# One decoder kernel: every low weight part on VectorE, the token norm's sums one step earlier, the decay products in one place, state keys scaled on ScalarE, two half output tiles placed among the last transposes

## Chip, cores and metric

The kernel runs on one core of a Trainium2 chip. The metric is the device time of one execution in microseconds, the median of several runs; lower is better. The engines are named as in the profile: PE (TensorE matrix products), PEld (its weight loads), DVE (VectorE), ACT (ScalarE), POOL (GpSimd) and SP (SyncE, which issues the transfers of weights).

## Reference

A decoder trunk of two layers on 512 tokens of width 1024, all in float32. Each layer adds three blocks to the residual stream:

```python
for layer in range(DEPTH):                       # DEPTH = 2
    x = x + 0.5 * swiglu(rmsnorm(x, norm_ffn1[layer]), ...)      # D_FF = 2816
    x = x + hybrid_mixer(rmsnorm(x, norm_mix[layer]), ...)
    x = x + 0.5 * swiglu(rmsnorm(x, norm_ffn2[layer]), ...)
return rmsnorm(x, norm_final)
```

The mixer makes one input projection and feeds three groups of heads: HGRN2 (a gated linear recurrence; q, forget gate f, value i and output gate g, 4 heads of 64), a gated delta rule (q, k, v through a causal convolution of 4 taps and SiLU, gates `g = -exp(a_log) * softplus(gd_a + dt_bias)` and `beta = sigmoid(gd_b)`, a triangular solve per chunk, 4 heads of 128), and RG-LRU (a scan). Their outputs are normed, gated, concatenated to 1024 columns and multiplied by `w_out`.

## The kernel before

**Products.** A float32 product is done as three products of split operands: each weight block has a high part `whi` and a low part `wlo`, each activation a high and a low part; `mm3_step` issues hi by hi (L212), hi by lo (L213) and lo by hi (L214), each 128x512. One weight unit (128 columns of outputs, 8 blocks of 128 inputs) is 24 such matmuls. Activations lie with features on partitions and the 512 tokens along the row.

**Weights.** SP loads a raw unit (`wraw`, three buffers). `_split` makes, for each half of a unit, `whi` by a copy on ACT (L176) and `wlo` by a subtraction (L177) on `self.lo_engine`: DVE in the feed-forward blocks, the value projection and the output projection, POOL during the rest of the mixer's input stage. A half is prepared one unit ahead of its use.

**Order.** In the mixer the order of PE is written by hand (`manual_schedule(engines={PE})`); the other engines' orders are made by the framework's scheduler. `Slots` runs a main list of projections, each of which yields a step after every 6 matmuls, and side lines (`sl.add`) that wait for an event and a number of steps: `("gd4", GAP)` resumes a line GAP steps after the projection of `gd4` is through. Whatever a line issues on PE when it is resumed stands at that place in PE's queue.

**The mixer's stages on PE.** (1) The value projection: 4 quarters q, tokens on partitions, 256 columns of HGRN2 values and 8 columns of gates into `pv` (L533 to L535). `rstd` (L293 and the small steps behind it) sums the squares for the norm's factor `rt`; `spread` (L304) puts it on all partitions as `rb` (L306), by which every projection's result is multiplied on DVE. (2) Projections gd4 to gd7 (keys), with a side line for the gates: `log1pexp` (L404 to L419, some 30 operations on 128x16, nearly all on DVE), L615 (three sums of g), L617 (their exponentials) and four decay products L626 with exponential (L628) and mask (L629); and a side line for the keys: transposes (L641), key products (L667, multiplied by DT on DVE, L668). When all four heads are through, L686 scales the result and `gdn_solve` sends its 16x16 blocks through DRAM and solves them on DVE (L745, L747, 15 pairs). (3) The two HGRN2 heads, hq1 first: L970 multiplies, L496 applies SiLU, and then come 8 levels of blocks (L1017 and L1004 on PE; L1022, L1008, L988 and L989 on DVE), the two heads alternating, with 6 matmuls of a projection between. (4) Convolved queries and values (L485, L492, L496; transposes again L641), merges of the solve (L777, L786), the chunk chain, gates. (5) The end: four transposes of the delta rule's output (L935), each multiplied (L505) and split (L235, L236) into parts of `Y`; then `mixer_out`, 8 output tiles of 24 matmuls, whose order over the parts of Y is `Y_ORDER = (0, 1, 6, 7, 2, 3, 4, 5)`.

`gtmp` tiles ("gt") have four buffers, PSUM banks "mm" and "mx" three each, "hx" two.

Of the kernel before, what the change touches and what calls it, by code (L numbers as in the profile page):

```python
# [5 lines left out]
F32 = mybir.dt.float32  # L6
# [106 lines left out]
class Trunk:  # L113
# [56 lines left out]
    def _split(self):  # L170
        raw, n = self.loaded[len(self.ready) // 2]
        o = n // 2 * (len(self.ready) % 2)
        hi = self.tile(self.wp, (P, NWU // 2), F32R, "whi")
        lo = self.tile(self.wp, (P, NWU // 2), F32R, "wlo")
        hi, lo, raw = hi[:, 0:n // 2], lo[:, 0:n // 2], raw[:, o:o + n // 2]
        self.nc.scalar.copy(hi, raw)  # L176
        self.lo_engine.tensor_tensor(lo, raw, hi.bitcast(F32), ALU.subtract)  # L177
        self.ready.append((hi, lo))
# [335 lines left out]
    def mixer_in(self, l):  # L514
# [8 lines left out]
        for q in range(4):  # L523
            w = self.weights()
            if q == 3:
                self.rt = self.rstd(0, NJ, "mx")
# [9 lines left out]
        self.lo_engine = nc.gpsimd  # L536

        def norm():
            for j in range(NJ):
                nc.vector.tensor_scalar(ba[:, j, :], pv[j][:, 256:264], self.rt[:, j:j + 1], None, ALU.mult)  # L540
            for j in range(NJ):
                nc.scalar.activation(HV[:, j, :], pv[j][:, 0:256], AF.Copy, scale=self.rt[:, j:j + 1])
            yield 1
            _, self.rb = self.spread(self.rt, NJ, "mm")
            sl.fire("rb")


        tl = lambda n, tag: self.tile(self.mp, (P, n), F32, tag)
        for line in (norm(), self.gdn_gates(l, ba), self.gdn_k(), self.gdn_q(), self.gdn_v(), self.gdn_core(),
# [9 lines left out]
        sl.run([(need and (need, 0), line) for _, need, line in main])  # L559

    def mixer_out(self, l, nxt):
        nc = self.nc
        self.lo_engine = nc.vector
# [31 lines left out]
    def gdn_gates(self, l, ba):  # L595
# [3 lines left out]
        yield ("rb", 0)  # L599
# [3 lines left out]
        nc.scalar.activation(v3(self.beta), ba[:, :, 0:4], AF.Sigmoid)  # L603
# [7 lines left out]
        nc.vector.tensor_tensor(v3(self.g), v3(sp), nea, ALU.mult)  # L611
        yield 7
# [9 lines left out]
        gm = None  # L622
        for c in range(NJ + 1):
            if c:
                pd = self.bank("mx")
                nc.tensor.matmul(pd, lhsT=self.gt, rhs=gm.rearrange("p a b -> p (a b)"), start=True, stop=True)  # L626
                dt = self.DT[:, 4 * c - 4:4 * c, :]
                nc.scalar.activation(dt.rearrange("p a b -> p (a b)"), pd, AF.Exp)  # L628
                nc.vector.tensor_tensor(dt, dt, self.le[:, None, :].to_broadcast([P, 4, P]), ALU.mult)  # L629
            if c < NJ:  # L630
                gm = self.gtmp()
                nc.vector.tensor_tensor(gm, self.le[:, None, :].to_broadcast([P, 4, P]),
                                        bc(self.g[:, 4 * c:4 * c + 4], P), ALU.mult)
                yield 1
# [17 lines left out]
    def gdn_k(self):  # L652
# [17 lines left out]
        for h in range(4):  # L670
# [254 lines left out]
    def gdn_out(self, l):  # L925
# [4 lines left out]
        yield 3  # L930
        for h in range(4):
            yield (f"z{h}", 0)
# [176 lines left out]
    def hgrn_out(self, l, V):  # L1109
# [4 lines left out]
        for i in range(2):  # L1114
# [6 lines left out]
            self.out_parts(i, pt.rearrange("p a b -> p (a b)"), self.hgg[i], self.par[:, c0 + C_HGW:c0 + C_HGW + 1])  # L1121

# [20 lines left out]
    def rglru(self, l):  # L1143
# [35 lines left out]
        for i in range(2):  # L1179
            self.parts(6 + i, bx[i])  # L1180


    def run(self):
        tc, nc, t = self.tc, self.nc, self.t
        from contextlib import ExitStack
        with ExitStack() as es:
# [8 lines left out]
            self.lo_engine = nc.vector  # L1195
# [64 lines left out]
GAP = 3  # L1260
# [78 lines left out]
```

## Time and profile before

| | |
|---|---|
| median of 3 runs | 2126.92 us (2125.84 to 2127.35) |
| the profiled execution | 2125.51 us, its span 2123.7 us |
| PE busy | 2074.2 us, 98% of the span |
| DVE, ACT, POOL busy | 1122.3, 807.3 and 159.6 us |
| mean granted TensorE clock | 0.991 of full speed |

The profile is of one execution. Busy time of PE counts matmuls whose ends are modelled, so waits of PE are read from the list of waits, which names for each group of waiting instructions who released it, and the stretches of lower clock from windows that give the granted clock (PEclk). In the timeline each row has its start, its duration, the engine, the line and operation, tiles and, in brackets, the idle time before it and its releaser.

### The profile page before, as it was taken

What the parts mean: (1) busy time and instruction counts of PE and PEld (TensorE: products, weight loads), DVE (VectorE), ACT (ScalarE), POOL (GpSimd) and SP (SyncE); (2) the same over time, 40 slices, a digit from 0 to 9 for tenths busy, and PEclk for the clock granted to TensorE, in tenths of its full rate; (3) what the DMA queues carried; (4) which work ended last, traced back from release to release, by engine and by line L of the source; (5) the groups of instructions that cost most, each with busy time, mean ns of one, the idle gap of its engine ahead of it and who ended that gap; (6) DMA issues with size and microseconds to landing.
All of it is one profiled execution on the core that took longest, in us unless ns stands there. A gap on an engine that the chain in (4) does not pass through costs nothing.

```text
span 2123.7 us, 26758 instructions
## 1 busy us (share of the span) xinstructions
PE 2074.2 (98%) x10292; PEld 1681.8 (79%) x10292; DVE 1122.3 (53%) x1996; ACT 807.3 (38%) x1519; POOL 159.6 (8%) x148
## 2 busy tenths in 40 slices
PE   8999999899999999999999999998899999999997
PEld 6888888778778788888888888887688778888886
DVE  6434445686475543444644343457855754444445
ACT  5323224544464332323433232346345543223233
POOL 0000000332230000000000000003312200000000
PEclk9999999999999999999999999999999999999998
DMA  5232222221113223232223232222211222322222
GB/s 182 91 98 95 94 98 77 85 71 45 51 60 96 93 90 100 90 99 91 98 90 100 90 100 90 94 79 85 66 41 51 70 90 99 92 98 93 96 90 70
DMA packets 67488, 184.99 MB, mean 87 GB/s; under 512 B 18976, under 2 KB 21920, under 8 KB 67360
## 3 DMA queue, kind: packets, MB, share of 16 engines
q1 hardware_dynamic: 66128, 182.12, 26.9%
q8 instruction: 81, 1.33, 0.2%
q10 hardware_dynamic: 1232, 1.16, 0.2%
q14 instruction: 47, 0.39, 0.1%
HBM read 180.36 MB, written 2.88 MB: 86 GB/s over the span
## 4 chain that ended last, share of the span: by engine, by line
PE 92%; DVE 6%; ACT 1%; DMA 0%; issue 0%; SPq 0%; DVEq 0%; ACTq 0%
PE mm L212 13%; PE mm L213 12%; PE mm L214 12%; PE mx L212 8%; PE mx L214 8%; PE mx L213 8%; PE hx L212 8%; PE hx L214 8%; PE hx L213 8%; DVE tmp L492 1%; PE hx L1004 1%; PE mx L641 1%; PE hx L1059 0%; DVE r_q L911 0%; PE hx L1062 0%
## 5 line engine op out<-in xcount | busy, mean ns | idle before, releaser
L176 ACT CAST whi<-wraw 128x512 fp32r<-128x512 f32 (+2 forms) x696 | 420.2, 606 | 983.7 <-PE mm L213 330.6
L177 DVE TENSOR_TENSOR wlo<-wraw,whi 128x512 fp32r<-128x512 f32 (+2 forms) x592 | 393.6, 666 | 316.2 <-ACT whi L176 315.3
L212 PE MATMUL mm<-xh,whi 128*128 128x512 f32 x1120 | 462.5, 413 | 6.6 <-ACT whi L176 6.6
L213 PE MATMUL mm<-xl,whi 128*128 128x512 f32 x1120 | 443.7, 396 | 0.0
L214 PE MATMUL mm<-xh,wlo 128*128 128x512 f32 x1120 | 443.4, 396 | 0.0
L212 PE MATMUL mx<-xh,whi 128*128 128x512 f32 x704 | 279.5, 397 | 0.0
L214 PE MATMUL mx<-xh,wlo 128*128 128x512 f32 x704 | 278.6, 396 | 0.0
L213 PE MATMUL mx<-xl,whi 128*128 128x512 f32 x704 | 277.0, 394 | 0.0
L212 PE MATMUL hx<-y,whi 128*128 128x512 f32 x692 | 273.0, 395 | 0.0
L213 PE MATMUL hx<-y,whi 128*128 128x512 f32 x692 | 272.1, 393 | 0.0
L214 PE MATMUL hx<-y,wlo 128*128 128x512 f32 x692 | 272.1, 393 | 0.0
L212 PEld LDWEIGHTS mm<-xh,whi 128*128 128x128 f32 x1120 | 212.6, 190 | 56.8 <-ACT whi L176 6.6
L214 PEld LDWEIGHTS mm<-xh,wlo 128*128 128x128 f32 x1120 | 212.4, 190 | 50.9 <-DVE wlo L177 0.2
L213 PEld LDWEIGHTS mm<-xl,whi 128*128 128x128 f32 x1120 | 213.1, 190 | 47.0 <-issue 3.4
L177 POOL TENSOR_TENSOR wlo<-wraw,whi 128x512 fp32r<-128x512 f32 x104 | 142.5, 1374 | 358.7 <-ACT whi L176 350.3
L214 PEld LDWEIGHTS mx<-xh,wlo 128*128 128x128 f32 x704 | 132.6, 188 | 32.6 <-issue 0.7
L213 PEld LDWEIGHTS mx<-xl,whi 128*128 128x128 f32 x704 | 132.8, 189 | 30.7 <-issue 0.2
L212 PEld LDWEIGHTS mx<-xh,whi 128*128 128x128 f32 x704 | 132.4, 188 | 31.1 <-issue 1.0
L214 PEld LDWEIGHTS hx<-y,wlo 128*128 128x128 f32 x692 | 130.1, 188 | 31.0
L213 PEld LDWEIGHTS hx<-y,whi 128*128 128x128 f32 x692 | 130.2, 188 | 30.6 <-DVE y L236 1.0
L212 PEld LDWEIGHTS hx<-y,whi 128*128 128x128 f32 x692 | 130.0, 188 | 29.5
L359 DVE SCALAR_TENSOR_TENSOR x<-hx,x 128x512 f32<-128x512 f32 x94 | 65.0, 692 | 132.8 <-PE hx L214 132.8
(328 smaller groups left out, 1910.4 us busy)
## 6 DMA issues: line engine op xcount, KB each, us to landing
wraw<-in_wgu SPq DMA_DIRECT2D x176, 512.0 KB, 3.7
wraw<-in_wd SPq DMA_DIRECT2D x64, 512.0 KB, 3.5
wraw<-in_win SPq DMA_DIRECT2D x52, 512.0 KB, 3.5
wraw<-in_wd SPq DMA_DIRECT2D x32, 384.0 KB, 3.0
wraw<-in_wout SPq DMA_DIRECT2D x16, 512.0 KB, 3.5
wraw<-in_wv SPq DMA_DIRECT2D x8, 264.0 KB, 2.5
x<-in_x SPq DMA_DIRECT2D x3, 512.0 KB, 7.9
out_dram<-xw SPq DMA_DIRECT2D x4, 256.0 KB, 2.5
```

The source lines that it names most:

```text
L176: self.nc.scalar.copy(hi, raw)
L177: self.lo_engine.tensor_tensor(lo, raw, hi.bitcast(F32), ALU.subtract)
L212: nc.tensor.matmul(ps, lhsT=a, rhs=xh, start=(n == 0), stop=False)
L213: nc.tensor.matmul(ps, lhsT=a, rhs=xl, start=False, stop=False)
L214: nc.tensor.matmul(ps, lhsT=b, rhs=xh, start=False, stop=(n == size - 1))
L359: nc.vector.scalar_tensor_tensor(xm, pd, 0.5, xm, ALU.mult, ALU.add)
L492: nc.vector.scalar_tensor_tensor(c, pad[:, 1 + i:1 + i + S], w[i], c, ALU.mult, ALU.add)
L641: self.nc.tensor.transpose(ps[:, c, :], v[:, c * P:(c + 1) * P], self.ident)
L1004: nc.tensor.matmul(banks[e][:, j], lhsT=k[r, j * P:(j + 1) * P], rhs=half(q)[r, j], start=True, stop=True)
```

## The change

1. `wlo` is always made on VectorE. Before, 104 halves (52 in each layer's mixer) were made on POOL.
2. `rstd` stands at the third quarter of the value projection (q == 2) and not at the fourth; `spread`, the scaling of the gate columns (`ba`) and of the HGRN2 values (`HV`) follow the projection at once and not in a side line one step later; the gates' line no longer waits for an event.
3. The decay products: all four masked tiles `gm` are computed right behind g, the four products stand together behind L615, and beta's sigmoid is issued behind them.
4. The keys that go into the states are scaled on ACT as they leave PSUM (three activations for each head), in place of a copy on ACT and three multiplications per layer on POOL (L694).
5. GAP is 4 and not 3; the delta rule's output line starts one step later and each of its heads waits 3 steps behind its gate z.
6. `out_first`, twice: the first 12 matmuls (parts 0, 1, 6, 7 of Y) of output tiles 0 and 1 go into the main list as soon as these parts are there (event "y"); `mixer_out` finishes the two tiles.

The number of matmuls is the same. The diff, cut to its core:

```diff
-        self.lo_engine.tensor_tensor(lo, raw, hi.bitcast(F32), ALU.subtract)
+        self.nc.vector.tensor_tensor(lo, raw, hi.bitcast(F32), ALU.subtract)
...
-            if q == 3:
+            if q == 2:
                 self.rt = self.rstd(0, NJ, "mx")
...
-        self.lo_engine = nc.gpsimd
-
-        def norm():
-            for j in range(NJ):
-                nc.vector.tensor_scalar(ba[:, j, :], pv[j][:, 256:264], self.rt[:, j:j + 1], None, ALU.mult)
-            for j in range(NJ):
-                nc.scalar.activation(HV[:, j, :], pv[j][:, 0:256], AF.Copy, scale=self.rt[:, j:j + 1])
-            yield 1
-            _, self.rb = self.spread(self.rt, NJ, "mm")
-            sl.fire("rb")
+        _, self.rb = self.spread(self.rt, NJ, "mm")
+        for j in range(NJ):
+            nc.vector.tensor_scalar(ba[:, j, :], pv[j][:, 256:264], self.rt[:, j:j + 1], None, ALU.mult)
+        for j in range(NJ):
+            nc.scalar.activation(HV[:, j, :], pv[j][:, 0:256], AF.Copy, scale=self.rt[:, j:j + 1])
...
+        main += [(("y", 0), self.out_first()) for _ in range(2)]
+        sl.run(main)
+
+    def out_first(self):
+
+        ps, w = self.bank(), self.weights()
+        for n in range(KT // 2):
+            self.mm3_step(ps, w, self.Y, n, KT, Y_ORDER[n])
+            if n % 2:
+                yield
+        self.first.append((ps, w))
...
-            ps = self.bank()
-            self.mm3(ps, self.weights(), self.Y, Y_ORDER)
+            if m < len(self.first):
+                ps, w = self.first[m]
+                for n in range(KT // 2, KT):
+                    self.mm3_step(ps, w, self.Y, n, KT, Y_ORDER[n])
+            else:
+                ps = self.bank()
+                self.mm3(ps, self.weights(), self.Y, Y_ORDER)
...
-        nc.scalar.activation(v3(self.beta), ba[:, :, 0:4], AF.Sigmoid)
...
+        gm = []
+        for c in range(NJ):
+            gm.append(self.gtmp())
+            nc.vector.tensor_tensor(gm[c], self.le[:, None, :].to_broadcast([P, 4, P]),
+                                    bc(self.g[:, 4 * c:4 * c + 4], P), ALU.mult)
         yield 7
...
-        gm = None
-        for c in range(NJ + 1):
...
+        for c in range(NJ):
+            pd = self.bank("mx")
+            nc.tensor.matmul(pd, lhsT=self.gt, rhs=gm[c].rearrange("p a b -> p (a b)"), start=True, stop=True)
+            dt = self.DT[:, 4 * c:4 * c + 4, :]
+            nc.scalar.activation(dt.rearrange("p a b -> p (a b)"), pd, AF.Exp)
+            nc.vector.tensor_tensor(dt, dt, self.le[:, None, :].to_broadcast([P, 4, P]), ALU.mult)
+        nc.scalar.activation(v3(self.beta), ba[:, :, 0:4], AF.Sigmoid)
         sl.fire("DT")
...
-            nc.scalar.copy(hc(self.Kn)[:, h], ps[:, 0:NJ - 1, :])
             yield ("DT", 1)
+            for c in range(NJ - 1):
+                nc.scalar.activation(self.Kn[:, 4 * c + h, :], ps[:, c, :], AF.Copy,
+                                     scale=self.ex[:, 1, 4 * c + h:4 * c + h + 1])
...
-        for c in range(NJ - 1):
-            cs = slice(4 * c, 4 * c + 4)
-            kd = self.Kn[:, cs, :]
-            nc.gpsimd.tensor_tensor(kd, kd, bc(self.ex[:, 1, cs], P), ALU.mult)
...
-        yield 3
+        yield 4
         for h in range(4):
-            yield (f"z{h}", 0)
+            yield (f"z{h}", 3)
...
+        yield ("hgy", 0)
+        self.sl.fire("y")
...
-GAP = 3
+GAP = 4
```

Where this moves instructions is seen in the engines' queues. First PE around the gates, before: L615 sums g, "mx" are PSUM banks, "gt" the masked tiles, and a "..." stands for three more rows of the same projection.

```order
L214 MATMUL mm_3158<-xh_91,wlo_3107 128x512
L615 MATMUL mx_3175<-g_3079,cst_87 128x16 x3
L212 MATMUL mm_3158<-xh_91,whi_3106 128x512
L213 MATMUL mm_3158<-xl_92,whi_3106 128x512
L214 MATMUL mm_3158<-xh_91,wlo_3107 128x512
...
L626 MATMUL mx_3192<-gt_3184,cst_87 128x512
L212 MATMUL mm_3158<-xh_91,whi_3110 128x512
L213 MATMUL mm_3158<-xl_92,whi_3110 128x512
L214 MATMUL mm_3158<-xh_91,wlo_3111 128x512
...
L626 MATMUL mx_3204<-gt_3196,cst_87 128x512
```

The same place after; L628 is the former L615, L637 the former L626, L648 the key transposes that were L641.

```order
L214 MATMUL mm_3110<-xh_91,wlo_3024 128x512
L628 MATMUL mx_3154<-g_3068,cst_87 128x16 x3
L637 MATMUL mx_3163<-gt_3070,cst_87 128x512
L637 MATMUL mx_3167<-gt_3072,cst_87 128x512
L637 MATMUL mx_3171<-gt_3074,cst_87 128x512
L637 MATMUL mx_3175<-gt_3076,cst_87 128x512
L648 MATMUL mx_3180<-cst_87,y_596_3100 128x128 x4
L212 MATMUL mm_3190<-xh_91,whi_3113 128x512
```

Before, the first key transposes stood 30 projection matmuls behind L304 and L615 12 matmuls behind them, with the four decay products after it, 6 matmuls apart; after, L304 is followed by 48 projection matmuls, then L615's successor, the four products in a row and the first transposes.

The second place is DVE ahead of the first HGRN2 level, before: L683 and L686 belong to the delta rule's solve, L961, L991 and L970 to head hq1.

```order
L683 TENSOR_TENSOR bk_3396<-bk_3396,beta_3043 128x16
L961 TENSOR_SCALAR gd_v_3365<-gd_v_3365 128x512
L686 TENSOR_TENSOR y_575_3027<-y_575_3027,bk_3396 128x512 x4
L991 TENSOR_TENSOR hg_tot_3632<-gd_v_3365 128x256
L970 TENSOR_TENSOR gd_v_3365<-mm_3492,rb_3041 128x512
L991 TENSOR_TENSOR hg_tot_3673<-hg_tot_3632 128x128
```

The same place after (L975 was L970, L692 was L683, L695 was L686).

```order
L697 SCALAR_TENSOR_TENSOR ik_3428<-ksq_3080,rk_3404 128x16
L975 TENSOR_TENSOR gd_v_3360<-mm_3378,rb_3006 128x512
L692 TENSOR_TENSOR bk_3421<-bk_3421,beta_3033 128x16
L177 TENSOR_TENSOR wlo_3597<-wraw_3535,whi_3596 128x512
L695 TENSOR_TENSOR y_592_3078<-y_592_3078,bk_3421 128x512 x4
L177 TENSOR_TENSOR wlo_3601<-wraw_3535,whi_3600 128x512
L1027 TENSOR_TENSOR gd_v_3360<-hx_3564,cst_87 128x512
```

hq1's multiplication now stands ahead of the four scalings of the solve, and halves of `wlo` stand among them. Further on, in the levels, DVE has this piece after (L1013 was L1008, L750 and L752 were L745 and L747):

```order
L1013 COPY_PREDICATED hg_s_703_3585<-cst_87,hx_3749 128x256
L752 TENSOR_TENSOR gt_3441<-gt_3441,solve_3474 128x5x11
L492 SCALAR_TENSOR_TENSOR tmp_3742<-tmp_3739,par_76,tmp_3742 128x512
L750 TENSOR_TENSOR solve_3477<-gt_3430,gt_3441 128x4x12
L492 SCALAR_TENSOR_TENSOR tmp_3742<-tmp_3739,par_76,tmp_3742 128x512
L752 TENSOR_TENSOR gt_3441<-gt_3441,solve_3477 128x4x12
L492 SCALAR_TENSOR_TENSOR tmp_3742<-tmp_3739,par_76,tmp_3742 128x512
L750 TENSOR_TENSOR solve_3480<-gt_3430,gt_3441 128x3x13
L1013 COPY_PREDICATED hg_s_704_3586<-cst_87,hx_3750 128x256
```

Before, the two copies of a level (L1008) of this head stood next to each other, or with one solve step between; here three steps of a convolution stand between them too.

The third place is PE's end of the mixer, before: the last transposes L935 and the first output tile, whose operands are parts of Y (`y_...`).

```order
L214 MATMUL mm_5322<-xh_91,wlo_5275 128x512
L935 MATMUL mx_5359<-cst_87,r_q_3733 128x128 x4
L212 MATMUL mm_5369<-y_976_5092,whi_5325 128x512
L213 MATMUL mm_5369<-y_976_5092,whi_5325 128x512
L214 MATMUL mm_5369<-y_976_5092,wlo_5326 128x512
```

The same place after (L940 was L935); the "..." stands for the other rows of the first half of tile 0.

```order
L214 MATMUL mm_5318<-xh_91,wlo_5271 128x512
L212 MATMUL mm_5364<-y_976_5097,whi_5321 128x512
...
L212 MATMUL mm_5387<-y_976_5097,whi_5367 128x512
L213 MATMUL mm_5387<-y_976_5097,whi_5367 128x512
L214 MATMUL mm_5387<-y_976_5097,wlo_5368 128x512
...
L940 MATMUL mx_5404<-cst_87,r_q_3738 128x128 x4
L212 MATMUL mm_5387<-y_1000_5219,whi_5367 128x512
```

The last transposes stood ahead of all 192 matmuls of the output stage; now 18 of these stand ahead of them. The first L935 of a layer, which stood 36 projection matmuls behind the chunk chain's last products, stands 48 behind them.

## Rows read from the trace of the kernel before

**Rows 1.** The page: busy time (us), share and instruction count of each engine.

```profile
PE 2074.2 (98%) x10292; PEld 1681.8 (79%) x10292; DVE 1122.3 (53%) x1996; ACT 807.3 (38%) x1519; POOL 159.6 (8%) x148
```

**Rows 2.** Waits of PE, whole span: line, releaser: us in total, times, longest.

```profile
PE mx L641 <- ACT y L496: 12.4, 2, 6.3
...
PE mx L935 <- DVE r_q L911: 4.6, 6, 1.3
PE hx L1017 <- ACT gd_v L496: 4.4, 2, 2.2
...
PE hx L1004 <- DVE solve L745: 3.2, 2, 2.2
PE hx L1004 <- DVE gt L747: 1.9, 1, 1.9
PE mx L641 <- ACT tmp L496: 1.8, 4, 0.6
...
PE hx L1004 <- DVE hg_k L989: 1.1, 2, 0.6
PE hx L1004 <- DVE hg_s L1022: 1.1, 2, 0.8
```

**Rows 3.** Windows: length, busy us of PE, PEld, DVE, ACT, POOL; PEclk, DMA.

```profile
405.40:412.20 6.80, 3.63 (x11) 3.05 (x12) 5.31 (x13) 3.24 (x12) 0.98 (x1) 0.50 0.24 80
...
1682.00:1685.40 3.40, 3.40 (x12) 2.72 (x11) 1.44 (x2) 0.45 (x1) 0.00 (x0) 0.50 0.00 0
```

**Rows 4.** Timeline of layer 0 from the gates to the first key transposes.

```profile
396.40 1.28 ACT L404 ACT_TABLE_LOAD   x1
397.69 0.22 ACT L404 ACTIVATE sp_z<-sp_a 128x16 f32<-128x16 f32 x1
...
398.98 3.82 POOL L177 TENSOR_TENSOR wlo<-wraw,whi 128x512 fp32r<-128x512 f32 x3 [6.07 <-ACT whi L176]
399.07 1.25 DVE L414 TENSOR_TENSOR sp_r<-sp_r,sp_w 128x16 f32<-128x16 f32 x1
...
403.56 0.17 DVE L414 TENSOR_TENSOR sp_r<-sp_r,sp_w 128x16 f32<-128x16 f32 x1
...
408.57 1.12 PE L641 MATMUL mx<-cst,y 128*128 128x128 f32 x4 [6.31 <-ACT y L496]
```

**Rows 5.** Timeline behind them: sums of g, exponential, decay product.

```profile
413.52 0.74 PE L615 MATMUL mx<-g,cst 128*128 128x16 f32 x6
...
415.04 0.21 ACT L617 ACTIVATE gex<-mx 128x48 f32<-128x48 f32 x1
...
415.58 1.02 PE L626 MATMUL mx<-gt,cst 128*128 128x512 f32 x2
```

**Rows 6.** Timeline ahead of the levels: two projection matmuls, the solve's scaling, hq1.

```profile
441.55 0.39 PE L213 MATMUL mm<-xl,whi 128*128 128x512 f32 x1
...
441.78 0.40 PE L214 MATMUL mm<-xh,wlo 128*128 128x512 f32 x1
...
445.75 2.48 DVE L686 TENSOR_TENSOR y<-y,bk 128x512 f32<-128x512 f32 x4
...
448.49 0.68 DVE L970 TENSOR_TENSOR gd_v<-mm,rb 128x512 f32<-128x512 f32 x1
```

**Rows 7.** Window over layer 0's levels, columns as in rows 3.

```profile
450.00:490.00 40.00, 37.05 (x288) 28.57 (x290) 34.32 (x88) 12.49 (x27) 11.61 (x10) 0.92 0.31 73
```

**Rows 8.** Timeline within the levels: first solve step, one convolution step.

```profile
457.72 0.24 DVE L745 TENSOR_TENSOR solve<-gt,gt 128x15 f32<-128x15 f32 x1
...
479.24 0.75 DVE L492 SCALAR_TENSOR_TENSOR tmp<-tmp,par,tmp 128x512 f32<-128x512 f32 x1
```

**Rows 9.** Groups of the page: low parts by engine: busy us, mean ns | idle before.

```profile
L177 DVE TENSOR_TENSOR wlo<-wraw,whi 128x512 fp32r<-128x512 f32 (+2 forms) x592 | 393.6, 666 | 316.2 <-ACT whi L176 315.3
...
L177 POOL TENSOR_TENSOR wlo<-wraw,whi 128x512 fp32r<-128x512 f32 x104 | 142.5, 1374 | 358.7 <-ACT whi L176 350.3
```

**Rows 10.** Timeline at the mixer's end: the output's scaling by its norm.

```profile
627.34 4.69 DVE L911 TENSOR_TENSOR r_q<-r_q,ro 128x512 f32<-128x512 f32 x4
```

More of the change, by code (lines that the diff above doesn't have):

```diff
@@ L535, in mixer_in @@
                     nc.tensor.matmul(pv[j], lhsT=xl, rhs=a, start=False, stop=(k == KT - 1))
-        self.lo_engine = nc.gpsimd
-        def norm():
-            for j in range(NJ):
-                nc.vector.tensor_scalar(ba[:, j, :], pv[j][:, 256:264], self.rt[:, j:j + 1], None, ALU.mult)
-            for j in range(NJ):
-                nc.scalar.activation(HV[:, j, :], pv[j][:, 0:256], AF.Copy, scale=self.rt[:, j:j + 1])
-            yield 1
-            _, self.rb = self.spread(self.rt, NJ, "mm")
-            sl.fire("rb")
-        tl = lambda n, tag: self.tile(self.mp, (P, n), F32, tag)
-        for line in (norm(), self.gdn_gates(l, ba), self.gdn_k(), self.gdn_q(), self.gdn_v(), self.gdn_core(),
+        _, self.rb = self.spread(self.rt, NJ, "mm")
[3 more added lines that the diff above has]
+            nc.scalar.activation(HV[:, j, :], pv[j][:, 0:256], AF.Copy, scale=self.rt[:, j:j + 1])
+        for line in (self.gdn_gates(l, ba), self.gdn_k(), self.gdn_q(), self.gdn_v(), self.gdn_core(),
                      self.hgrn(1, HV), self.hgrn(0, HV), self.hgrn_norm(HV), self.rglru(l), self.hgrn_out(l, HV),
@@ L558, in mixer_in @@
         main.sort(key=lambda m: m[0])
-        sl.run([(need and (need, 0), line) for _, need, line in main])
+        self.first = []
+        main = [(need and (need, 0), line) for _, need, line in main]
+        main += [(("y", 0), self.out_first()) for _ in range(2)]
[7 more added lines that the diff above has]
+        self.first.append((ps, w))
     def mixer_out(self, l, nxt):
         nc = self.nc
-        self.lo_engine = nc.vector
         self.norm_begin()
         for m in range(KT):
-            ps = self.bank()
-            self.mm3(ps, self.weights(), self.Y, Y_ORDER)
+            if m < len(self.first):
[5 more added lines that the diff above has]
+                self.mm3(ps, self.weights(), self.Y, Y_ORDER)
             xm = self.x[:, m, :]
@@ L598, in gdn_gates @@
         sl = self.sl
-        yield ("rb", 0)
         c0 = l * NPC
@@ L621, in gdn_gates @@
         self.DT = self.tile(self.mp, (P, 16, P), F32, "DT")
-        gm = None
-        for c in range(NJ + 1):
[L624 to L634, printed above, removed]
+        for c in range(NJ):
[5 more added lines that the diff above has]
+        nc.scalar.activation(v3(self.beta), ba[:, :, 0:4], AF.Sigmoid)
         sl.fire("DT")
@@ L1121, in hgrn_out @@
             self.out_parts(i, pt.rearrange("p a b -> p (a b)"), self.hgg[i], self.par[:, c0 + C_HGW:c0 + C_HGW + 1])
+        self.sl.fire("hgy")
     def in_rx(self, l, i):
@@ L1194, in run @@
             self.dp = pool("dram", 2, space=bass.MemoryType.DRAM)
-            self.lo_engine = nc.vector
             self.plan_weights()
```

## The prediction

> **What bounds the kernel now.** I read the page first. PE is busy for 98% of the span, DVE for 53%, ACT for 38%, POOL for 8% [rows 1]. The change leaves PE's matmuls as they are, so all it can win is time in which PE stands still or runs slowly. The second view is therefore the list of PE's waits. Of its rows the change can reach 30.5 us: 12.4 for the first key transposes, 4.6 for the output's transposes, 4.4 for the first HGRN2 level of hq1, 7.3 in the levels that follow (3.2 + 1.9 + 1.1 + 1.1), 1.8 for four other transposes [rows 2]. That makes 12.4 + 4.6 + 4.4 + 7.3 + 1.8 = 30.5; the other waits, at the start, the end and the blocks' norms, stay.
>
> The third view is the windows, for the granted clock. [...] Waits and low clock together: 30.5 + 10.1 = 40.6 us. If all of it went, the profiled execution would come to 2125.5 - 40.6 = 2084.9 us. The profiled one is 1.4 us below the median of 2126.92, so on the scale of the median this is 2086.3, the floor of what follows.
>
> By stage, two layers together, with the low clock behind each wait (shares of the 10.1 us by the windows' busy times): first key transposes 12.4 + 3.3; first level of hq1 4.4 + 1.7 (one layer only shows it); the later levels 7.3 + 3.4; the other transposes 1.8; the end 4.6 + 1.7.
>
> **Part by part.**
>
> *The gates and the first key transposes.* The timeline shows why the 6.3-us wait stands where it does [rows 4]. The chain of small steps of `log1pexp` and the convolution of gd4 share DVE's queue; PE's transposes need the convolution's SiLU. While POOL makes three low halves in a row (3.82 us), a step on 128x16 takes 1.25 us, with POOL quiet the same step takes 0.17 us: each POOL half costs a DVE step some 1.08 us more. [...] After the change POOL makes no halves, `rstd` is done a quarter of the value projection earlier, L304 follows the projection at once, and the transposes stand 48 and no longer 30 projection matmuls behind it, 18 x 0.23 = 4.1 us later (a matmul of 128x512 starts 0.23 us after the one before [rows 6]). Against 6.3 us of wait there are 4.1 us of other PE work, three stretched steps at 1.08 (3.2 us), and the decay products ahead of the transposes, 4 x 1.02 = 4.1 us [rows 5]. Together 11.4 against 6.3 plus what is new on DVE: some four halves of `wlo` at 0.67 us, 2.7 us [rows 9], and four masked tiles at about the 0.7 us of other 128x512 steps [rows 6], 2.8 us. That is 11.4 against 11.8: the old wait goes but for about half a microsecond.
>
> The new wait would be at L615, which now stands ahead of the transposes and needs g, the last of the small steps. I price it at 0.6 us a layer, between 0 and the 3 us by which the sum above is out if no stretched step is saved. The four decay products pass through three PSUM banks, and the third needs L617 done: L617 ends 1.73 us behind the start of L615 (413.52 to 415.25), the third product comes 0.74 + 2 x 1.02 = 2.78 us behind it [rows 5], so nothing is added. [...]
>
> Gain: 12.4 + 3.3 - 1.2 = 14.5 us.
>
> *First level of hq1.* Its SiLU waits for L970, which stood on DVE behind the solve's four scalings (2.48 us from 445.75) and started at 448.49 [rows 6]. After the change it stands ahead of them. PE's wait of 2.2 us in either layer [rows 2] is less than these 2.48 us, so it goes; gain 4.4 + 1.7 = 6.1 us. What comes later is the solve: its scalings end about a multiplication and a `wlo` half later, and its last key product 6 matmuls later, some 2.7 us in all. The first solve step ran at 457.72 [rows 8]; in DVE's order after it stands a level further on, so nobody waits for that at once.
>
> *The levels.* DVE is busy for 34.3 of 40 us there, POOL for 11.6 [rows 7]. POOL's eight halves leave; DVE gets about six of them in the same time, 6 x 0.67 = 4.0 us a layer, and loses about as many stretched steps, 6 x 1.08 = 6.5 us at most, less where POOL's op met no DVE step. I count load and relief as equal. The waits for solve steps (3.2 + 1.9) come from solve steps and `wlo`-stretched steps ahead of the level's own; with the solve one level later I count them gone. The rows for hg_k and hg_s (1.1 us a layer together) I count as staying. And the new piece of order, three convolution steps between the two copies of a level, costs between 0 and 3 x 0.75 = 2.25 us a layer [rows 8]; on an engine busy for 86% I take 1.8. So 2.9 us a layer stay, and a low clock behind one of them is as likely as not: half of 1.7, or 0.85. Gain: 7.3 + 3.4 - 2 x 2.9 - 2 x 0.85 = 3.2 us.
>
> *The other transposes.* GAP 4 puts them a step of 6 matmuls later, 1.39 us; the longest of the four waits is 0.6 us [rows 2]. Gain 1.8 us.
>
> *The end.* The output's transposes wait for L911, four steps in 4.69 us [rows 10], against 4 x 0.68 = 2.7 us by the like step L970 [rows 6]. With 12 more matmuls ahead (2.8 us) against a longest wait of 1.3 [rows 2] the waits go. The last transposes now stand only 15 matmuls, 3.5 us, ahead of the products that use their result; the multiplication and the two parts of Y behind them are three steps of about 0.7 us, 2.1 us, with room of 1.4. Gain 4.6 + 1.7 = 6.3 us.
>
> *What is counted at nothing or as a remainder.* Scaling keys on ACT: ACT is busy for 12.5 of the tightest 40 us [rows 7], and the POOL multiplication that goes was awaited by nobody. 104 halves move to DVE, 104 x 0.67 = 70 us more on an engine that has 1000 us free [rows 1, 9]; each half is made a unit ahead of its use, which at 24 matmuls a unit is some 5.5 us and more, so a queue of a few microseconds on DVE hides. For halves that come late all the same, and for the closer end, I take 0.5 us a layer off.
>
> Sum: 14.5 + 6.1 + 3.2 + 1.8 + 6.3 - 1.0 = 30.9 us. Median after: 2126.9 - 30.9 = 2096.0 us. If the terms that I chose between bounds (0.6, 1.8, 0.85, 0.5) all lie at one end, it is 2090 or 2102.
>
> **Rivals.**
>
> *Everything goes.* If the levels too run without a wait and the clock never falls, 2086. For it: with POOL gone, no small step of DVE is stretched any more [rows 4]. Against: DVE stays at 34 of 40 us in the levels.
>
> *DVE becomes the bound of the levels.* The six halves a layer come as 4.0 us on top and the relief counts for nothing: the 7.3 + 3.4 us stay and 8 us are added, in place of the gain of 3.2. The sum falls by 3.2 + 8.0 to 19.7: 2107. For it: 34.3 of 40 us busy. Against: POOL's 11.6 us, during which DVE's steps are long, go at the same time.
>
> *The gates' wait moves to L615.* If g is as late as the convolution was, the 12.4 + 3.3 us stay in another row, the gain of 14.5 falls away: 30.9 - 14.5 = 16.4, or 2110.5. For it: g is the last of some 30 dependent steps, and halves of `wlo` stand between them. Against: 4.1 us more PE work ahead and no stretched steps.
>
> *Waits only move.* If gates, hq1 and levels give what they take and only the end and the four transposes win: 6.3 + 1.8 = 8.1, 2119; with the closer end lost too, no change.
>
> *Slower.* PE waits for low parts. From 104 halves a mean lateness of 30.9 / 104 = 0.30 us eats the gain, and (30.9 + 4.3) / 104 = 0.34 us makes it slower by 0.2%, over 2131. It would show as waits of PE or its weight loads for `wlo`. For it: `wlo` stands in DVE's queue in the order of the scheduler, behind solve steps. Against: over 5 us of lead for each half.
>
> **How the numbers follow.** 0.2% of 2126.9 is 4.3 us, about what a measurement of this kernel can tell from no change. Chances: the forecast (2090 to 2102) 0.55, everything goes 0.10, DVE the bound of the levels 0.13, the gates' wait moved 0.09, waits only move 0.08 (of this 0.03 below 2122.7 and 0.05 within the bound), slower 0.05 (0.01 of it within the bound). Faster: 0.55 + 0.10 + 0.13 + 0.09 + 0.03 = 0.90; the same 0.06; slower 0.04. The range goes from 2087, just above the floor, to 2112, so that it holds the two rivals at 2107 and 2110 and leaves out the last two and the lowest edge.
>
> **What would show it.** In the waits of the profile after: no row of 6 us for key transposes and none above 3 us at L615's successor; the row for the first level gone; rows for the levels of some 6 us in all; the output transposes' row gone. In the windows: PEclk of 0.50 in at most two or three stretches and not six. POOL's groups lose `wlo`, and 128x16 steps on DVE stand at 0.17 to 0.25 us throughout. The prediction is wrong if a row of several microseconds for `wlo` appears, if L615 waits for g as long as the transposes did, or if the levels' waits grow beyond today's 7.3 us.

## The result, and the profile after

The changed kernel takes 2089.11 us (median of 4 runs, 2088.65 to 2093.96) where the kernel before takes 2127.14 us: a ratio of 0.9826, 95% interval 0.9809 to 0.9843, or 38.0 us less. Forecast were 2096.0 us and a range of 2087 to 2112. The profiled execution took 2088.65 us, its span is 2086.6 us, 37.1 us less than before. Its executions come at two times, near 2089 and near 2094 us, and the granted clock tells them apart (0.996 and 0.993); what that may be stands in the last section.

The page first: busy time, share and count of each engine, as in [rows 1], and the group of the low halves, as in [rows 9].

```profile
PE 2063.3 (99%) x10292; PEld 1676.2 (80%) x10292; DVE 1118.8 (54%) x2100; ACT 807.2 (39%) x1533; POOL 12.6 (1%) x38
...
L177 DVE TENSOR_TENSOR wlo<-wraw,whi 128x512 fp32r<-128x512 f32 (+2 forms) x696 | 464.8, 669 | 347.3 <-ACT whi L176 344.5
```

DVE makes 104 halves more, 71.2 us of work (464.8 against 393.6), and its busy time falls by 3.5 us. So some 75 us of DVE's time before were no work at all but steps held up, 0.7 us for each of the 110 operations on 128x512 that POOL has lost (104 halves and 6 multiplications). The steps on 128x16 show it singly: of the 146 float32 ones on DVE, 26 took 0.48 to 1.29 us before, and none takes more than 0.26 us after.

The waits of PE over the whole span, to be read against [rows 2]:

```profile
PE mm L212 <- ACT whi L176: 6.7, 1, 6.7
PE hx L1009 <- DVE gt L752: 4.0, 2, 2.0
PE hx L304 <- DVE sq L302: 3.9, 1, 3.9
PE hx L293 <- DVE ssq L273: 1.5, 1, 1.5
PE hx L1009 <- DVE hg_s L1027: 0.4, 2, 0.2
```

Of the 30.5 us that the change could reach, 4.4 us are left, all in the levels. The windows of low clock, columns as in [rows 3], are two and not six, each behind one of the 2.0-us waits; the first row is the stretch of layer 0's levels, to be read against [rows 7].

```profile
440.00:480.00 40.00, 37.81 (x305) 28.86 (x305) 35.89 (x104) 14.08 (x30) 0.20 (x2) 0.96 0.28 63
465.10:468.50 3.40, 3.40 (x13) 2.25 (x10) 2.69 (x10) 0.39 (x1) 0.00 (x0) 0.50 0.24 77
1496.00:1499.40 3.40, 3.40 (x12) 2.38 (x10) 2.79 (x11) 0.13 (x1) 0.00 (x0) 0.50 0.23 77
```

The account of the span's 37.1 us: waits 30.5 - 4.4 = 26.1; low clock 10.1 - 3.4 = 6.7 (an estimate: half of PE's busy time in the stretches, 20.1 us before and 6.8 us after, at a granted clock of 0.50); the remaining 4.3 us are PE's own time. The page shows the last without a wait list: PE's busy time falls by 10.9 us, of which 6.7 are the low clock.

Three places of the timeline. The gates, in layer 0: g (L619) is done at 402.46, its sums (L628) start at 402.61, the four products run in a row and the key transposes (L648) follow; against [rows 4] and [rows 5].

```profile
402.29 0.17 DVE L619 TENSOR_TENSOR g<-g_sp,nea 128x16 f32<-128x16 f32 x1
...
402.61 0.81 PE L628 MATMUL mx<-g,cst 128*128 128x16 f32 x6
...
403.33 3.67 PE L637 MATMUL mx<-gt,cst 128*128 128x512 f32 x8
...
406.84 0.60 PE L648 MATMUL mx<-cst,y 128*128 128x128 f32 x4
```

Ahead of the levels, against [rows 6]: hq1's multiplication (L975) runs ahead of the solve's scalings, which end at 438.67, as the first level (L1022) starts.

```profile
434.89 0.69 DVE L975 TENSOR_TENSOR gd_v<-mm,rb 128x512 f32<-128x512 f32 x1
...
436.18 2.49 DVE L695 TENSOR_TENSOR y<-y,bk 128x512 f32<-128x512 f32 x4
...
438.62 1.16 PE L1022 MATMUL hx<-gd_v 64*128 64x128 f32 x16
```

In the levels, the wait that is left:

```profile
460.58 0.73 DVE L1013 COPY_PREDICATED hg_s<-cst,hx 128x256 f32<-128x256 int32 x1
...
461.23 0.72 DVE L492 SCALAR_TENSOR_TENSOR tmp<-tmp,par,tmp 128x512 f32<-128x512 f32 x1
...
462.78 0.75 DVE L492 SCALAR_TENSOR_TENSOR tmp<-tmp,par,tmp 128x512 f32<-128x512 f32 x1
...
463.55 0.72 DVE L1013 COPY_PREDICATED hg_s<-cst,hx 128x256 f32<-128x256 int32 x1
...
464.33 1.25 PE L1009 MATMUL hx<-gd_v 64*128 64x64 f32 x14 [1.99 <-DVE gt L752]
```

Each of these matmuls of plain float32 leaves two records, as the four products L637 leave 8. The first matmul of this part of the level had run at 461.90; the next one needs the second PSUM bank "hx", which the second copy frees at 464.27, and the others stand behind it. Between the two copies stand the three steps of a convolution. The list names a solve step (L752) as the releaser since it ended next to the copy.

### The profile page after: what moved, and what is told of

Read it like the earlier page. It is cut to its first block, busy times and chain, and to the rows that moved or that the text cites. A ratio compares the mean times of both kernels' runs of the same rounds, so it can differ in the third digit from the quotient of the medians.

```text
span 2086.6 us, 26732 instructions
## 1 busy us (share of the span) xinstructions
PE 2063.3 (99%) x10292; PEld 1676.2 (80%) x10292; DVE 1118.8 (54%) x2100; ACT 807.2 (39%) x1533; POOL 12.6 (1%) x38
## 4 chain that ended last, share of the span: by engine, by line
PE 98%; DVE 1%; DMA 0%; issue 0%; ACT 0%; DVEq 0%; SPq 0%; ACTq 0%
PE mm L212 14%; PE mm L214 14%; PE mm L213 14%; PE mx L212 8%; PE mx L214 8%; PE mx L213 8%; PE hx L212 8%; PE hx L214 8%; PE hx L213 8%; PE hx L1009 1%; PE mx L648 1%; PE hx L1064 1%; PE hx L1067 0%; PE mx L637 0%; PE mx L894 0%; PE mx L782 0%
## 5 line engine op out<-in xcount | busy, mean ns | idle before, releaser
L177 DVE TENSOR_TENSOR wlo<-wraw,whi 128x512 fp32r<-128x512 f32 (+2 forms) x696 | 464.8, 669 | 347.3 <-ACT whi L176 344.5
L212 PE MATMUL mm<-xh,whi 128*128 128x512 f32 x1120 | 456.0, 407 | 6.7 <-ACT whi L176 6.7
L213 PEld LDWEIGHTS mx<-xl,whi 128*128 128x128 f32 x704 | 132.7, 189 | 30.9 <-issue 0.2
L213 PEld LDWEIGHTS hx<-y,whi 128*128 128x128 f32 x692 | 130.2, 188 | 30.9 <-DVE y L236 1.1
L342 DVE TENSOR_TENSOR fu<-mx,rb 128x512 f32<-128x512 f32 x88 | 60.9, 692 | 139.7 <-PE mx L214 139.7
```

Source lines behind the costliest of these rows:

```text
L177: self.nc.vector.tensor_tensor(lo, raw, hi.bitcast(F32), ALU.subtract)
L212: nc.tensor.matmul(ps, lhsT=a, rhs=xh, start=(n == 0), stop=False)
L213: nc.tensor.matmul(ps, lhsT=a, rhs=xl, start=False, stop=False)
L342: nc.vector.tensor_tensor(u, pu, rb, ALU.mult)
```

## Experiments

**Which part brings the gain.** Two runs take the change apart at the low halves. In the first everything stays but the halves go back to POOL (112 of them: the 104, and 8 for the two half output tiles, which now fall into that stage):

```diff
-        self.nc.vector.tensor_tensor(lo, raw, hi.bitcast(F32), ALU.subtract)
+        self.lo_engine.tensor_tensor(lo, raw, hi.bitcast(F32), ALU.subtract)   # gpsimd in the mixer's input stage
```

> The kernel after, with the low halves of the mixer's input stage made on POOL again; everything else stays. Theory 'stretched steps' (POOL's halves lengthen DVE's 128x16 steps from 0.17 to 1.25 us and so the chain of the gates): the wait at the sums of g or at the first key transposes comes back with 2 to 6 us a layer, L911's successor takes 4 us and more again, and the time is 2097 to 2108 us. Rival 'order' (48 projection matmuls ahead of the gates' products, in place of 30 ahead of the transposes, are what hides the chain): no wait above 1 us at these places, and the levels, with six halves less on DVE, wait no more than now (4.4 us); 2086 to 2092 us.

Measured: 2122.36 us, ratio to the kernel before 0.9979 (0.9970 to 0.9988). Nearly all of the gain is gone. Its waits of PE:

```profile
PE mx L639 <- ACT DT L641: 7.7, 2, 3.9
...
PE hx L1024 <- ACT gd_v L496: 5.7, 2, 2.9
PE mx L860 <- DVE state L891: 4.0, 2, 2.0
...
PE hx L1011 <- DVE hg_s L1029: 2.9, 4, 1.2
PE hx L1011 <- DVE solve L752: 2.9, 2, 1.5
PE mx L639 <- DVE gt L625: 2.7, 4, 0.9
```

The gates cost time again, now at the decay products (L639), with hq1 and the levels. But it is not the wait that the theory named: the sums of g have no row. Late are the masked tiles (L625, four in 4.65 us in layer 0) and the exponentials (L641), which free the products' PSUM banks; in layer 0 the first exponential starts only at 411.04, behind a SiLU and another step of the key convolution in ACT's queue. The time is higher than the theory's own 2097 to 2108 us. The orders of DVE and ACT are not quite those of the kernel after: the scheduler, which chooses them, puts hq1's multiplication behind the solve's scalings again. So this run mixes held steps with another order; the runs with idle operations further on do not.

The second run is the kernel before with this one edit and nothing else (PE's order stays; the scheduler's orders of DVE and ACT move with it):

```diff
-        self.lo_engine.tensor_tensor(lo, raw, hi.bitcast(F32), ALU.subtract)
+        self.nc.vector.tensor_tensor(lo, raw, hi.bitcast(F32), ALU.subtract)
```

> The kernel before, with nothing changed but that every low half is made on DVE. Theory 'stretched steps': the 6.3-us wait of the first key transposes falls to 3 us or less in each layer, the waits for the output's scaling (L911, 4.6 us in all) go, and the time is 2108 to 2118 us. Rival 'order': the wait stays above 5 us in each layer, the levels wait longer by the six halves (4 us a layer), and the time is 2122 to 2135 us.

Measured: 2093.4 us, ratio 0.9840 (0.9826 to 0.9855), better than either theory had it. This one moved operation is worth 32.4 us against the kernel before beside it (2125.8 us); the whole change was worth 38.0 us.

```profile
PE mx L641 <- ACT y L496: 3.7, 2, 1.9
...
PE mx L641 <- ACT tmp L496: 1.2, 2, 0.6
PE hx L1004 <- DVE gt L747: 0.6, 2, 0.3
PE hx L1004 <- DVE hg_k L989: 0.6, 2, 0.3
```

The key transposes wait 3.7 us where they waited 12.4; the rows for hq1 and for the end of the mixer are gone, though hq1's multiplication stands behind the four scalings here too. What the other parts add together does not show in the medians: the ratio of the whole change is 0.9826 beside the result and 0.9841 in its second measurement below, and this run's 0.9840 lies between. The spans of the profiled executions differ by 4.4 us (2091.0 and 2086.6).

**By what mechanism POOL cost time.** POOL's halves could have cost time by holding up DVE or by coming late and shifting the order. So the next two runs leave the kernel after as it is, with the same order on DVE, ACT and PE (the traces agree in it, instruction by instruction), and add an operation on POOL for each half made in that stage, 112 in all, that nobody waits for but the buffer's next load:

```diff
         self.nc.vector.tensor_tensor(lo, raw, hi.bitcast(F32), ALU.subtract)
+        if self.extra:                       # mixer's input stage
+            self.nc.gpsimd.tensor_tensor(raw, raw, hi.bitcast(F32), ALU.subtract)
```

> The kernel after, with a subtraction on POOL for each of the 104 low halves added that nobody needs: it overwrites the raw half with raw - high once DVE has made its low half. The order of DVE, ACT and PE is that of the kernel after. Theory 'stretched steps' (POOL's subtractions, by running, hold up DVE): DVE's 128x16 steps take 1.2 us beside them again, the waits of the gates, of hq1 and of the levels come back, and the time is 2110 to 2130 us. Rival 'late halves or order' (what cost time before was that POOL delivered low halves later, or held places in the order): nobody waits for these subtractions, so 2088 to 2092 us.

Measured: 2126.1 us, ratio 0.9992 (0.9981 to 1.0002): the whole gain is gone, by work whose result is thrown away. The timeline at the gates and the row of the waits:

```profile
399.13 1.29 POOL L179 TENSOR_TENSOR wraw<-wraw,whi 128x512 f32<-128x512 f32 x1 [3.09 <-DVE sp_r L417]
...
399.17 1.28 DVE L416 TENSOR_TENSOR sp_r<-sp_r,sp_w 128x16 f32<-128x16 f32 x1
```

```profile
PE mx L632 <- DVE g L623: 8.6, 2, 4.3
```

The step on 128x16 starts 0.04 us behind POOL's operation and ends with it: 1.28 us for what takes 0.17. The sums of g, which were just in time in the kernel after, wait 4.3 us in each layer. Over the whole kernel DVE's busy time rises from 1118.8 us, by 50.7 us, with the same 2100 instructions:

```profile
PE 2085.5 (98%) x10292; PEld 1689.4 (79%) x10292; DVE 1169.5 (55%) x2100; ACT 806.1 (38%) x1533; POOL 161.6 (8%) x150
```

That the time is that of the kernel before is chance, for the account is another. PE's waits in the stages that the change touches are 20.6 us here and 30.5 us before, but the low clock costs 22.7 us and not 10.1 (45.4 us of PE's busy time lie in stretches at 0.50, one of them 20 us long in layer 0's levels). The row of hq1, which the theory expected too, is not back: its multiplication keeps its new place ahead of the solve's scalings.

In the sister run POOL fills the raw half with zeros:

```diff
+            self.nc.gpsimd.memset(raw, 0.0)
```

> As the run with subtractions that nobody needs, but POOL fills the raw half with zeros in their place: it writes as much and reads nothing. If any POOL operation on 128x512 holds up DVE, 2100 us and more; if it takes two operands read by POOL, the 128x16 steps of two operands keep their 0.17 us and the time is 2088 to 2093 us. [...]

Measured: 2090.19 us, ratio 0.9831 (0.9818 to 0.9845): as the kernel after.

```profile
398.30 0.53 POOL L179 MEMSET wraw<- 128x512 f32 x1 [3.95 <-DVE wlo L177]
...
398.36 0.17 DVE L416 TENSOR_TENSOR sp_r<-sp_r,sp_w 128x16 f32<-128x16 f32 x1
```

The same step runs under the fill at its 0.17 us. So in these two runs the DVE step of two operands was held up (1.28 us) beside a POOL operation that reads two operands, and not (0.17 us) beside one that writes as much and reads nothing.

The fill is not free for every step. All six steps of one SBUF operand on 128x16 that began beside a fill (L257, which is L255 in the kernel after) ended only with it, 0.34 to 0.58 us in place of 0.17:

```profile
434.29 0.53 POOL L179 MEMSET wraw<- 128x512 f32 x1 [3.66 <-DVE wlo L177]
...
434.44 0.41 DVE L257 TENSOR_SCALAR rs_p<-rs_s 128x16 f32<-128x16 f32 x1
```

That is 1.6 us of DVE's time in all (two steps directly behind a held one took 0.07 us more), and no wait of PE came of it.

**The early sums.** In the kernel after, the sums of the token norm go back to the last quarter:

```diff
-            if q == 2:
+            if q == 3:
```

> The kernel after with the sums of the token norm at the last quarter of the value projection (q == 3), as before; the rest stays. The chain of the gates then begins some 24 matmuls of 128x264 later, about 3 us, against PE work that stays. If that chain sets the place of the gates' products (the prediction priced a wait of 0 to 3 us a layer there), PE waits 1 to 4 us a layer at the sums of g: 2091 to 2100 us. If it has 3 us to spare, the time is that of the kernel after, 2088 to 2094 us.

Measured: 2104.54 us, ratio 0.9902 (0.9884 to 0.9919), 15 us above the kernel after.

```profile
PE mx L628 <- DVE g L619: 8.9, 2, 4.4
```

That is more than either theory allowed. `spread` waits too (L304, 0.7 us a layer), and the clock falls for 6.8 us behind each wait at the gates and for 10.2 us in layer 0's levels. In the new order of PE the gates' chain has no time to spare, as 402.46 against 402.61 said, and the early sums are what the new place of L628 rests on.

**The key transposes a step earlier.** GAP stays 4 except for the keys:

```diff
-            yield (f"gd{4 + h}", GAP)
+            yield (f"gd{4 + h}", GAP - 1)
```

> The kernel after with the key transposes one step (6 matmuls) earlier, as GAP 3 had it, and GAP 4 for the others. The solve then begins about 1.4 us earlier and DVE's order has the two copies of each level next to each other or with one solve step between. Theory 'split copies': the 2.0-us wait in each layer's levels goes and with it the low clock behind it, no new wait of over 0.5 us at the key transposes, 2081 to 2085 us. Rival 'DVE is full': a wait of 1 us or more turns up one level later, or at the key transposes, and the time stays at 2087 to 2091 us.

Measured: 2095.65 us, ratio 0.9854 (0.9841 to 0.9867). Both theories missed the time. The 2.0-us wait of the levels went as the first had it, and the clock never falls before the kernel's end, but other waits came, at the key transposes and in the levels as the rival had it and elsewhere, more than went:

```profile
PE mx L648 <- ACT y L496: 2.4, 3, 1.1
PE mx L637 <- ACT DT L639: 2.0, 2, 1.0
PE mx L782 <- issue: 2.0, 2, 1.0
PE mx L782 <- DVE gt L774: 1.9, 2, 0.9
PE hx L1009 <- DVE hg_k L994: 1.8, 2, 0.9
...
PE mx L637 <- ACT gex L630: 1.0, 2, 0.5
PE hx L1009 <- DVE solve L750: 0.7, 2, 0.3
```

Here the transposes stand ahead of L628, and the decay products wait for their PSUM banks (1.0 + 0.5 us a layer), what the prediction had looked at for the kernel after and found to fit there.

**The half output tiles.** They are left out; the last transposes stand ahead of all 192 output matmuls again:

```diff
-        main += [(("y", 0), self.out_first()) for _ in range(2)]
```

> The kernel after without the two half output tiles: the last transposes stand ahead of all 192 output matmuls again, the others stay where they are. If the half tiles are what hides the output's norm and scaling, PE waits for the scaled output again by 1 to 2 us a layer, with a stretch of low clock behind it at the end of layer 1's mixer: 2092 to 2097 us. If the quicker scaling (no POOL op beside it) and the 12 projection matmuls more ahead of the first transposes already hide it, no such row appears and the time is within 2 us of the kernel after.

Measured: 2091.44 us (2090.17 to 2095.12), ratio 0.9837 (0.9822 to 0.9851). Its waits of PE are those of the kernel after, row by row within 0.1 us; no row for the output's scaling. The half tiles bring nothing that these runs can tell.

**The state keys on POOL again**, with a copy on ACT and three multiplications a layer:

```diff
+            nc.scalar.copy(hc(self.Kn)[:, h], ps[:, 0:NJ - 1, :])
             yield ("DT", 1)
-            for c in range(NJ - 1):
-                nc.scalar.activation(self.Kn[:, 4 * c + h, :], ps[:, c, :], AF.Copy,
-                                     scale=self.ex[:, 1, 4 * c + h:4 * c + h + 1])
...
+            nc.gpsimd.tensor_tensor(kd, kd, bc(self.ex[:, 1, cs], P), ALU.mult)
```

> The kernel after with the state keys copied on ACT and multiplied on POOL again, three operations of two SBUF operands a layer at 1.0 us. Nobody awaits them, but each can hold up one or two DVE steps by a microsecond, ahead of the levels: 0 to 3 us a layer if the scaling of the solve or hq1 stand beside them, so 2089 to 2095 us; nothing, 2088 to 2091 us, if no step of the gates' or the solve's chain meets them.

Measured: 2092.35 us, ratio 0.9847 (0.9832 to 0.9862). One row is new, in each layer's first levels:

```profile
PE hx L1011 <- DVE gd_v L988: 1.6, 2, 0.8
```

So this part is worth 0.8 us of wait a layer; the medians alone would not show it.

**What the last wait is made of.** The convolution of the first query head is issued later, by one, two or three steps of 6 matmuls:

```diff
-        then(ps)
+        if event == "gd0":
+            def line():
+                yield (event, 2)             # 3 in the third run
+                then(ps)
+            self.sl.add(line())
+        else:
+            then(ps)
```

In the run with one step `then(ps)` stands behind the last `yield` of the projection, to the same effect.

> The kernel after with one edit: the convolution of the first query head is issued one step later, so that DVE has the two copies of an HGRN2 level next to each other and the three convolution steps behind them. Theory 'split copies' (the 2.0-us wait that is left in each layer's levels is the second PSUM bank, freed late because three steps of 0.75 us stand between the two copies): the wait of 2 x 2.0 us and both stretches of low clock go, 7 to 8 us less, 2080 to 2083 us. Rival 'DVE is full' (36 of 40 us busy): the same wait turns up one level later, and the time stays at 2087 to 2091 us.

> The kernel after with the convolution of the first query head issued two steps later: DVE has the two copies of the level and also that head's two multiplications ahead of the first convolution step. With one step the wait only moved to the next level (1.3 us in each layer). If it is the three convolution steps of 2.25 us that somebody has to wait for, two steps take them behind both levels: no wait of over 0.5 us in the levels, and nothing new at the first query transposes, which had 4.9 us to spare with one step: 2081 to 2084 us where no stretch of low clock comes without a wait, some 5 us more where one does. If DVE is simply full, 1 us or more a layer stays: 2085 us and more.

> As with two steps, one more. The last convolution step then stands behind the copies of the next level but one, and its SiLU ends close to the first query transposes. Not full: 2081 to 2084 us, with at most 0.5 us of wait at those transposes. Full: a wait of 1 us or more a layer there or in the levels, 2085 us and more.

Measured: 2087.68 us (2085.41 to 2089.97), 2087.24 us (2087.03 to 2087.85) and 2083.7 us (2083.38 to 2087.27); ratios 0.9812 (0.9796 to 0.9829), 0.9825 (0.9811 to 0.9840) and 0.9812 (0.9797 to 0.9827). The row of the levels in the three, one fence for each kernel:

```profile
PE hx L1012 <- DVE gt L755: 2.7, 2, 1.3
```

```profile
PE hx L1028 <- DVE gd_v L1000: 1.9, 2, 1.0
```

```profile
PE hx L1028 <- DVE gd_v L1000: 1.5, 2, 0.7
```

With the two copies side by side the wait of 2.0 us went and one of 1.3 us came a level later; then 1.0, then 0.7, each time elsewhere. Both theories hold in part. The convolution between the copies was the place, and DVE, at 36 of 40 us in this stretch, is short of time by 0.7 us a layer or more in each of the four places tried. In the third run no stretch of low clock follows either. The kernel with three steps is the fastest of all: three of its four executions took 2083.4 to 2083.9 us, where the kernel after takes 2088.7 to 2089.4 in the better of its two times. That it is faster than the kernel after is not shown, though: the kernel before took 2124.06 us beside it, 3 us less than beside the result, its interval overlaps that of the kernel after, and its ratio is that of the run with one step.

**The scale.** The kernel after once more, beside the runs with idle POOL operations:

> The kernel after itself, beside the others on the same chip: 2088 to 2091 us by every theory; it is the scale for runs that differ by a few us.

Measured: 2093.94 us (2089.15 to 2094.26), ratio 0.9841 (0.9827 to 0.9854); two executions at 2089 and three at 2094 us, so the median jumps with the draw, here out of the expected 2088 to 2091. Differences of less than 5 us between two medians above are therefore read from the rows of the waits.

## Why the prediction was right, point by point

The low clock first. The sum's 3.3, 1.7, 3.4 and 1.7 us are shares of 10.1 us, and the floor of 2086.3 us rests on them too. No run shows 10.1 us of lost time as such. The trace before shows PE busy for 20.1 us in six stretches at a granted clock of 0.50 (0.51 in one), and 10.1 is half of that, an estimate. The sum over the six windows, and two pairs of neighbouring projection matmuls, the first outside the stretches and the second within:

```profile
sum 27.20, PE 20.14 PEld 16.07 DVE 19.15 ACT 9.37 POOL 4.54; mean PE 3.36 PEld 2.68 DVE 3.19 ACT 1.56 POOL 0.76
```

```profile
461.54 0.39 PE L213 MATMUL mm<-xl,whi 128*128 128x512 f32 x1
461.77 0.39 PE L214 MATMUL mm<-xh,wlo 128*128 128x512 f32 x1
...
468.65 0.63 PE L213 MATMUL mm<-xl,whi 128*128 128x512 f32 x1
469.08 0.63 PE L214 MATMUL mm<-xh,wlo 128*128 128x512 f32 x1
```

They start 0.23 and 0.43 us apart. By this spacing the estimate is 20.1 x 0.20 / 0.43 = 9.4 us before and 3.2 after, and PE's own time below would be larger by some 0.5 us.

- *The gates and the key transposes.* Forecast 14.5 us, measured 15.7: the 12.4 us, the 3.3 us of low clock behind them, and no wait at L628, where 0.6 us a layer were priced. g came 0.15 us ahead. The sum of this step had three causes side by side (more PE work ahead, no stretched steps, earlier sums), and it counted three stretched steps, where the trace before has four in each layer's chain, 1.2 us each. The runs weigh the causes: without POOL's halves alone 8.7 of 12.4 us go; with the new order but idle subtractions on POOL 8.6 us come at the sums of g; without the early sums 8.9 us come there.
- *hq1.* Forecast 6.1 us, measured 6.1. The reason given, its place ahead of the solve's scalings, is only half of it: the run with the low halves alone on DVE has the old place and no wait. The run with idle subtractions has the new place and POOL at work, and no row for hq1 either. So each of the two, the new place and the unstretched steps, is enough by itself.
- *The levels.* Forecast were 2.9 us of wait and 0.85 us of low clock a layer, measured 2.2 and 1.7. The new piece of order was priced at 1.8 us a layer and costs 2.0; the 1.1 us of hg_k and hg_s that I let stay shrank to 0.2. The fall of the clock that I took as likely as not came in both layers.
- *The other transposes and the end.* Forecast 1.8 and 6.3 us, measured 1.8 and 6.3. At the end the price was right and its reason not: with L911's successor at 2.49 us for its four steps, where it took 4.69 [rows 10], the wait is gone without the half tiles and without the 12 matmuls ahead, as the runs without half tiles and with the low halves alone show.
- *The remainder.* 1.0 us for late low halves was not needed: no wait for `wlo` stands in the list.
- *What was missing: 4.3 us of PE's own time.* The prediction held PE's work to be the same. PE's busy time, low clock taken out, is 2074.2 - 10.1 = 2064.1 us before and 2063.3 - 3.4 = 2059.9 us after. In the run with the low halves alone it is 2063.7 (2065.4 busy, one stretch of low clock of 3.4 us), so POOL's halves alone do not bring it. But the new order alone does not either: in the run with idle subtractions, with PE's order of the kernel after, it is 2085.5 - 22.7 = 2062.8, and in the run with the key transposes a step earlier, where the clock does not fall, 2062.8 as well. About 3 us of it need POOL quiet and the transposes at their new place. By what this happens stays open.

The sum: 30.9 forecast for the profiled execution, 37.1 in its span. Terms that were too low: gates 1.2, low halves 1.0, PE's own time 4.3; the levels 0.3 too high. The waits went as forecast; the weight was put on the order of PE where the runs put it on POOL. That the stages fit so well is in part luck: for hq1, the four other transposes and the end the forecast took the whole of the old rows, and any cause that clears a row gives the same sum. The measured 2089.1 us lies 2 us above the range's lower edge, and just below the band of 2090 to 2102 that had 0.55 of the chances. That band does not follow from the ends that the prediction states: with all four terms at nothing the sum gives 2088.5, and with 3, 2.25 and 1.7 us in place of 0.6, 1.8 and 0.85 it gives 2103.4. I counted DVE's new halves in the levels (4.0 us a layer) as equal to the steps that are no longer stretched; the page's 75 us over the whole kernel, against 71 us of new halves, bear that out for the sum, while in the levels the load is the larger (34.3 us busy of 40 before, 35.9 after), and yet all the waits but two rows are gone. A wait hangs on the few short steps of a chain that are hit, and these were stretched sevenfold, while a new half in the queue adds 0.7 us once.

## What to carry to other kernels

Before work is put on GpSimd to unburden a VectorE that is half idle, look at the shortest VectorE steps beside it: if a step of 0.17 us reads 1.25 us there, most of GpSimd's operation (here 1.08 us of a mean 1.37) is being paid for by VectorE, and by whatever hangs on that step. One added operation on the suspected engine, whose result nobody needs, tells contention from order in a single run, and one that writes as much and reads nothing tells which kind. When a rest of waits moves from place to place under small changes of order, the engine behind it may well be full there; whether less work on it helps was not tried here.

## What the runs showed of the hardware

- POOL's subtraction of two SBUF tiles held a DVE step until its own end (1.28 us beside 1.29 us); a fill on POOL of the same size (0.53 us) held no step of two operands (0.17 us for the same step), and held all six steps of one SBUF operand on 128x16 that began beside it, to its end (0.34 to 0.58 us in place of 0.17).
- The clock fell without any wait. In the run with the convolution two steps later PE was busy throughout, and the list has no wait in that region, and still the granted clock went to 0.50 for 10.3 us, which costs some 5 us (half of them, an estimate); in the 10 us before it PE ran, among others, matmuls on 32x32 tiles (64 records). Whether these bring the fall was not tried. The windows ahead of it, within it and behind it:

```profile
1530.00:1550.30 20.30, 20.30 (x189) 17.43 (x187) 13.51 (x31) 11.16 (x28) 0.10 (x1) 1.00 0.19 53
1550.30:1560.60 10.30, 10.30 (x35) 6.91 (x34) 0.37 (x2) 1.12 (x2) 0.00 (x0) 0.50 0.00 0
1560.60:1580.00 19.40, 19.40 (x259) 16.40 (x258) 14.30 (x32) 7.79 (x17) 0.20 (x2) 1.00 0.18 56
```

- Such a stretch without a wait also stands in the profile of the run with the convolution one step later, at 1552.6 to 1562.9 us. The 5 us between the two times of the kernel after look different. Its two profiled executions took 2088.65 and 2089.35 us and have 3.4 us of low clock behind each 2.0-us wait. The run with fills has its order of PE, DVE and ACT and its waits, and was profiled at 2093.95 us with the clock of 0.993: there 6.8 and 10.2 us stand behind the same two waits.

```profile
467.20:474.00 6.80, 6.80 (x59) 4.81 (x57) 4.28 (x11) 0.62 (x1) 1.09 (x3) 0.50 0.25 53
1498.00:1508.20 10.20, 10.20 (x75) 7.82 (x76) 6.01 (x19) 0.90 (x3) 1.09 (x3) 0.50 0.27 44
```

That is 10.2 us more of low clock, worth 5.1 us, the whole difference. The run without half tiles, profiled at 2092.69 us, has 3.4 and 10.3 us there. So the same wait is followed by a stretch of one length or another from execution to execution. For the kernel after itself this is inferred: no execution of it near 2094 us was profiled.
